# A hybrid encoder on one core: first activations on ScalarE's queue in two transfers, first weight pieces back to back on SyncE's, eight warm-up matmuls for eleven

## The chip, the core and the metric

The kernel runs on one NeuronCore of a Trainium2 chip. The core has five engines, each with its own instruction queue: TensorE (matmuls, with weight loads beside them), VectorE, ScalarE, GpSimd and SyncE, which here issues most of the DMAs. A DMA can be issued from the queue of SyncE, ScalarE or GpSimd; the issuing engine spends some time on it, and the transfer then runs on the core's DMA engines. The metric is the device time of one execution in microseconds.

## The reference

The input is 256 positions of width 2048, in float32. Two layers follow one another, each a token mixer and a gated MLP with residual adds, and a final RMS norm.

```python
h = x
for i in range(DEPTH):                        # DEPTH = 2
    hn = rms_norm(h, mix_norm[i])
    if i % 2 == 0: h = h + mixer_a(hn, ...)   # GQA, 16 query and 4 key heads, rotary
    else:          h = h + mixer_b(hn, ...)   # 3 groups of 8 heads, dilated windows
    h = h + conv_ffn(rms_norm(h, ffn_norm[i]), w_up, conv_w, conv_b, w_down)
return rms_norm(h, final_norm)
```

What matters here is the very first piece of this: the query, key and value projection of mixer A, `qkv = rms_norm(x) @ w_qkv` with a weight of 2048 x 3072. The kernel applies the norm's gain to x beforehand and its per-position factor after the projection, so the projection can begin as soon as some of x and some of the weight have been loaded.

## The kernel before

All matmuls of the projections compute a float32 product from parts: each operand is split into a high part, rounded to the matmul's input format, and a low part, the remainder. Three matmuls per tile are added up (high by high, high by low, low by high). The high part is a copy on ScalarE, the low part a subtraction on VectorE.

The activations come transposed from memory (`xT`, 128 partitions x 16 k-tiles x 256 positions). `load_xT(n)` loads four k-tiles, and `prep(j)` makes one k-tile's two parts: `split_scaled` on line 194 (ScalarE, the tile called xh in the profile) and line 197 (VectorE, the low part, under the same name). The weight comes in tiles of 512 x 512, that is 128 partitions x 2048 values or 1 MB. `feed` (line 121) loads one such tile (`raw`) and splits it in two halves, on line 146 (ScalarE, `wh`) and line 147 (VectorE, `wl`); lines 134 to 136 are its 24 matmuls, two blocks of 128 positions for each of four k-tiles, three matmuls each. Three `raw` buffers and three pairs of `wh` and `wl` go round.

`project2` computes the key block (n = 4) and the value block (n = 5) together, so that the first k-tiles of both can be used as they arrive. It passes a hook to `feed`. The first two tiles of each block are loaded in four pieces of 256 KB, the others in two of 512 KB, and the hook decides what is loaded beside them: for the first block, `load_xT(0)` to `load_xT(2)`, then parts of x and its sums of squares.

Within `feed` the splits of the weight are put into a high-priority block (`AHEAD`, 45 places), with which the framework's scheduler moves them ahead of work written earlier in the program. The order on each engine's queue is the one that results from that. For the first tile, the hook returns a function `mid`, which `feed` calls after each of its four pieces; `mid` issues the next activation piece and splits the present one.

Before all this, line 270 fills a tile with zeros and line 273 issues NWARM matmuls on it, whose result is not used. ScalarE's queue begins with the DMA of the gains (line 49) and a dummy activation (line 50, with the load of its function table ahead of it); GpSimd's has the DMA of an identity matrix (line 51).

Of the kernel before, what the change touches and what calls it, by code (L numbers as in the profile page):

```python
# [21 lines left out]
SCALE = 128.0 ** -0.5  # L22
NRAW, NHL = 3, 3
AHEAD = 45
NWARM = 11


@with_exitstack
def tile_encoder(ctx: ExitStack, tc: tile.TileContext, x, xT, w_a, w_ao, q_gain, k_gain, w_b, w_bo,
                 rel_bias, gains, w_up, conv, w_down, final_norm, rope, ident_c, onehot, out):  # L30
    nc = tc.nc
# [24 lines left out]
    def nm(s):  # L56
        uid[0] += 1
        return f"{s}_{uid[0]}"

    def ps_tile():  # L60
        return psp.tile([P, 512], F32, tag="ps", name=nm("ps"))
# [131 lines left out]
    def split_scaled(hi, lo, src, sc):  # L193
        nc.scalar.activation(hi, src, AF.Copy, scale=sc)
        if lo is None:
            return
        nc.vector.scalar_tensor_tensor(lo, src, sc, hi.bitcast(F32), ALU.mult, ALU.subtract)
# [15 lines left out]
    def new_hT(kt):  # L213
        t = hpool.tile([P, 2 * NT], F32R, tag=f"x{kt}", name=nm("xh"))
        return t[:, :NT], t[:, NT:], t
# [55 lines left out]
    wps = ps_tile()  # L271
    for _ in range(NWARM):
        nc.tensor.matmul(wps, warm[:, 0, :P], warm[:, 0, :], start=True, stop=True)
# [227 lines left out]
    def mixer_a():  # L501
        with tc.tile_pool(name="apool", bufs=1) as ap:
# [24 lines left out]
            def load_xT(n):  # L527
                xt = ap.tile([P, 4, NT], F32, tag=("qTh", "qTl", "vh", "vl")[n], name=nm("xt"))

                def load(j0, j1):  # L530
                    nc.sync.dma_start(xt[:, j0:j1, :], xT[:, 4 * n + j0:4 * n + j1, :])

                def prep(j):
                    kt = 4 * n + j
                    hT[kt] = new_hT(kt)
                    split_scaled(*hT[kt][:2], xt[:, j, :], gain[:, 0, kt:kt + 1])

                if n > 0:
                    load(0, 4)
                    for j in range(4):  # L540
                        prep(j)
                    return None
                load(0, 1)

                def mid(i):
                    if i < 3:
                        load(i + 1, i + 2)
                    prep(i)

                return mid  # L550

            def load_x(n):
                nc.sync.dma_start(h[:, :, n * 512:(n + 1) * 512],
# [3 lines left out]
            def hook(first_block, kg):  # L557
                if first_block and kg < 3:
                    return load_xT(kg)
                elif first_block:  # L560
                    load_x(2)
                    load_x(3)
                    rstd.append(finish_rstd(ss_in))
                elif kg == 0:
                    load_xT(3)
                elif kg == 1:
                    load_x(0)
                    tables()
                elif kg == 2:
                    load_x(1)  # L570
# [350 lines left out]
```

## Time and profile before

| | |
|---|---|
| median of 3 runs | 2316.41 us (2316.36 to 2316.6) |
| the profiled execution | 2316.06 us |
| its span, first to last instruction | 2313.9 us |
| TensorE busy (share of the span) | 2296.3 us (99%) |
| VectorE busy | 1603.5 us (69%) |
| ScalarE busy | 1199.2 us (52%) |
| bytes moved by DMA | 437.45 MB, mean 189 GB/s |

Times in the profile are microseconds from the start of the span. A row of the timeline has start, duration, engine, line, operation, what it writes and reads, how often; in brackets, how long the engine had been idle before and what ended that. "PE" is TensorE's matmul, "DVE" VectorE, "ACT" ScalarE, "POOL" GpSimd, "SPq" a DMA issue on SyncE's queue, "ACTq" one on ScalarE's. The chain of waits goes back from the last instruction, at each step to what released it. Matmuls overlap in the array: a row's 0.39 us is its whole way through, while the next one starts 0.23 us later. A row of a table of stretches has the stretch, its length, the busy time and number of instructions of TensorE, the weight load, VectorE, ScalarE and GpSimd, and then the granted clock, the share of time that the DMA engines were busy, and GB/s.

### The profile page before, as it was taken

Reading aid. Unit: us, or ns where it says so; the run is one execution under the profiler, and the core shown is the slowest. Engines: PE = TensorE matmul, PEld = TensorE weight load, DVE = VectorE, ACT = ScalarE, POOL = GpSimd, SP = SyncE. Lnnn points to the kernel's source line nnn. Section 1 sums busy time; section 2 is a strip of 40 time slices with the busy share of each in tenths; the row PEclk is TensorE's granted clock in tenths of the full one; section 3 lists DMA queues with packets and bytes.
Section 4 is the critical chain, followed back from the end, with each engine's and each line's share of the span. In section 5 each row is a group of like instructions: output and inputs, shape, how many; then the busy total and the mean of one; then the engine's idle time right before and its main releaser. Section 6 shows DMA issues by size and latency. Waiting matters only on the chain.

```text
span 2313.9 us, 30001 instructions
## 1 busy us (share of the span) xinstructions
PE 2296.3 (99%) x11641; PEld 1941.8 (84%) x11641; DVE 1603.5 (69%) x2197; ACT 1199.2 (52%) x1658; POOL 189.3 (8%) x143
## 2 busy tenths in 40 slices
PE   9999999999999999999999999999999999999997
PEld 7888788888888888888888888888888888888886
DVE  6877877775457776878866885677777744677754
ACT  6565465554345554545454554445555533555543
POOL 2330010100001010010000000001010100001010
PEclk9999999999999999999999999999999999999999
DMA  8434565765555555566555554556555555555553
GB/s 299 164 130 162 192 203 192 230 197 184 199 187 182 195 182 192 189 210 210 182 181 179 185 182 164 182 191 210 185 182 187 184 196 197 182 190 182 193 195 133
DMA packets 229023, 437.45 MB, mean 189 GB/s; under 512 B 10400, under 2 KB 193440, under 8 KB 201104
## 3 DMA queue, kind: packets, MB, share of 16 engines
q1 hardware_dynamic: 226976, 429.82, 55.1%
q0 software_dynamic: 1472, 5.15, 0.7%
q8 instruction: 91, 1.49, 0.3%
q10 hardware_dynamic: 432, 0.56, 0.1%
q14 instruction: 52, 0.43, 0.1%
HBM read 429.20 MB, written 6.29 MB: 188 GB/s over the span
## 4 chain that ended last, share of the span: by engine, by line
PE 92%; DVE 6%; issue 1%; ACT 1%; DMA 0%; SPq 0%; POOL 0%; POOLq 0%; DVEq 0%; ACTq 0%
PE acc L116 28%; PE acc L135 15%; PE acc L136 15%; PE acc L134 15%; PE acc L117 14%; DVE wl L147 2%; DVE tT L231 2%; PE ps L202 1%; PE ps L204 0%; PE ps L205 0%; PE ps L206 0%; PE ps L799 0%; DVE ro L583 0%; PE ps L653 0%; DVE ssq L591 0%
## 5 line engine op out<-in xcount | busy, mean ns | idle before, releaser
L116 PE MATMUL acc<-xh,wh 128*128 128x512 f32 x2816 | 994.2, 399 | 0.1
L117 PE MATMUL acc<-xh,wl 128*128 128x256 f32 x2816 | 789.3, 280 | 0.0
L147 DVE TENSOR_TENSOR wl<-raw,wh 128x1024 fp32r<-128x1024 f32 (+1 forms) x456 | 553.7, 1216 | 331.9 <-ACT wh L146 328.2
L146 ACT ACTIVATE wh<-raw 128x1024 fp32r<-128x1024 f32 (+1 forms) x456 | 475.6, 1045 | 551.8 <-PE acc L136 512.0
L116 PEld LDWEIGHTS acc<-xh,wh 128*128 128x128 f32 x2816 | 529.3, 188 | 130.6 <-DVE v L346 0.7
L111 DVE TENSOR_TENSOR wl<-raw,wh 128x1024 fp32r<-128x1024 f32 x352 | 431.1, 1225 | 207.1 <-ACT wh L110 202.9
L110 ACT ACTIVATE wh<-raw 128x1024 fp32r<-128x1024 f32 x352 | 372.5, 1059 | 327.0 <-PE acc L116 222.8
L117 PEld LDWEIGHTS acc<-xh,wl 128*128 128x128 f32 x2816 | 531.4, 189 | 1.0 <-issue 0.5
L135 PE MATMUL acc<-wl,ah 128*128 128x512 f32 x1024 | 399.6, 390 | 1.5 <-DVE wl L147 1.3
L134 PE MATMUL acc<-wh,ah 128*128 128x512 f32 x1024 | 399.3, 390 | 0.0
L136 PE MATMUL acc<-wh,al 128*128 128x512 f32 x1024 | 398.7, 389 | 0.0
L134 PE MATMUL acc<-wh,xh 128*128 128x512 f32 x768 | 303.1, 395 | 0.7 <-ACT wh L146 0.7
L135 PE MATMUL acc<-wl,xh 128*128 128x512 f32 x768 | 300.0, 391 | 0.2 <-DVE wl L147 0.2
L136 PE MATMUL acc<-wh,xh 128*128 128x512 f32 x768 | 299.3, 390 | 0.0
L135 PEld LDWEIGHTS acc<-wl,ah 128*128 128x128 f32 x1024 | 192.3, 188 | 43.7 <-DVE wl L147 4.6
L136 PEld LDWEIGHTS acc<-wh,al 128*128 128x128 f32 x1024 | 192.3, 188 | 39.7
L134 PEld LDWEIGHTS acc<-wh,ah 128*128 128x128 f32 x1024 | 192.3, 188 | 39.5
L365 POOL TENSOR_TENSOR cv<-cg,cv 128x512 f32<-128x512 f32 x44 | 98.8, 2245 | 1166.5 <-ACT wh L110 907.4
L136 PEld LDWEIGHTS acc<-wh,xh 128*128 128x128 f32 x768 | 144.2, 188 | 30.1
L135 PEld LDWEIGHTS acc<-wl,xh 128*128 128x128 f32 x768 | 144.4, 188 | 28.8 <-DVE wl L147 1.7
L134 PEld LDWEIGHTS acc<-wh,xh 128*128 128x128 f32 x768 | 144.5, 188 | 28.5 <-ACT wh L146 1.1
L190 ACT ACTIVATE ah<-cv 128x256 fp32r<-128x256 f32 x88 | 32.0, 410 | 108.8 <-POOL cv L365 108.8
(151 smaller groups left out, 1375.0 us busy)
## 6 DMA issues: line engine op xcount, KB each, us to landing
raw<-in_w_up_dram SPq DMA_DIRECT2D x352, 512.0 KB
raw<-in_w_down_dram SPq DMA_DIRECT2D x88, 1024.0 KB
raw<-in_w_b_dram SPq DMA_DIRECT2D x72, 1024.0 KB
raw<-in_w_bo_dram SPq DMA_DIRECT2D x24, 1024.0 KB
raw<-in_w_a_dram SPq DMA_DIRECT2D x16, 1024.0 KB
raw<-in_w_ao_dram SPq DMA_DIRECT2D x16, 1024.0 KB
raw<-in_w_a_dram SPq DMA_DIRECT2D x16, 256.0 KB
raw<-in_w_a_dram SPq DMA_DIRECT2D x8, 512.0 KB
```

Source lines behind the costliest of these rows:

```text
L110: nc.scalar.activation(wh, rk, AF.Copy)
L111: nc.vector.tensor_tensor(wl, rk, wh.bitcast(F32), ALU.subtract)
L116: nc.tensor.matmul(acc[j], wh[:, kt, c], x, start=first and i == 0 and kt == 0, stop=False)
L117: nc.tensor.matmul(acc[j][:, :NT], wl[:, kt, c], x[:, :NT], start=False, stop=last and i == len(kgs) - 1 and kt == 3)
L134: nc.tensor.matmul(accs[m], xh[:, c], wh[:, j, :], start=st, stop=False)
L135: nc.tensor.matmul(accs[m], xh[:, c], wl[:, j, :], start=False, stop=False)
L136: nc.tensor.matmul(accs[m], xl[:, c], wh[:, j, :], start=False, stop=sp)
L146: nc.scalar.activation(wh[:, c], r[:, c], AF.Copy)
L147: nc.vector.tensor_tensor(wl[:, c], r[:, c], wh[:, c].bitcast(F32), ALU.subtract)
L190: nc.scalar.activation(hi, src, AF.Copy)
L231: nc.vector.transpose(o[cols].rearrange("p a (m t) -> p a m t", m=2)[:, :, :, rows], s[rows].rearrange("p m (a c) -> p a m c", c=P)[:, :, ...
L365: nc.gpsimd.tensor_tensor(cv, cg, cv, ALU.mult)
```

## The change

`load_xT(0)` no longer loads its four k-tiles one by one, each between two weight pieces, on SyncE's queue. It issues them all at once from ScalarE's queue: the first k-tile (128 KB), then the other three in one transfer (384 KB). The function that `feed` calls after each weight piece is now `prep` alone, so the four weight pieces stand one behind the other on SyncE's queue. The calls of `prep` come in the same places as before; where the splits end up on ScalarE and VectorE is left to the scheduler. The warm-up has eight matmuls instead of eleven. The later tiles' loads keep their queue.

```diff
-NWARM = 11
+NWARM = 8
...
-                def load(j0, j1):
-                    nc.sync.dma_start(xt[:, j0:j1, :], xT[:, 4 * n + j0:4 * n + j1, :])
+                def load(j0, j1, q=nc.sync):
+                    q.dma_start(xt[:, j0:j1, :], xT[:, 4 * n + j0:4 * n + j1, :])
...
-                load(0, 1)
-
-                def mid(i):
-                    if i < 3:
-                        load(i + 1, i + 2)
-                    prep(i)
-
-                return mid
+                load(0, 1, nc.scalar)
+                load(1, 4, nc.scalar)
+                return prep
```

## The prediction

> **What bounds the kernel now.** I read the page first (busy shares and the chain that ended last), then the chain of waits over the first 50 us, then the timeline of the first 12 us.
>
> ```profile
> PE 2296.3 (99%) x11641; PEld 1941.8 (84%) x11641; DVE 1603.5 (69%) x2197; ACT 1199.2 (52%) x1658; POOL 189.3 (8%) x143
> ...
> PE 92%; DVE 6%; issue 1%; ACT 1%; DMA 0%; SPq 0%; POOL 0%; POOLq 0%; DVEq 0%; ACTq 0%
> ```
>
> TensorE is busy 99% of the span and 92% of the chain. Whatever delays its unbroken stream of matmuls at the start is paid once, in full, at the end, unless a later pause of TensorE takes it up. The edit touches only the start, so the question is when that stream begins.
>
> ```profile
> 1.66 0.42 SPq L531
> ...
> 2.12 5.11 DMA raw<-in_w_a_dram
> ...
> 7.26 0.64 ACT wh L146
> ...
> 7.92 0.70 DVE wl L147
> ...
> 8.67 0.50 PE acc L135
> 9.17 0.23 PE acc L136
> ...
> 45.59 0.24 PE acc L136
> ```
>
> This is the chain by time. The second weight piece, issued by SyncE at 2.12 us behind two activation pieces, lands at 7.23; its high part (ScalarE) and low part (VectorE) follow, and from 8.67 on the chain is one matmul after another, 0.23 us apart, up to 45.8 us. The timeline shows what came before that.
>
> ```profile
> 0.74 0.41 ACTq L49 DMA_DIRECT2D gain<-in_gains_dram  x1
> ...
> 1.46 4.28 PE L273 MATMUL ps<-warm 128*128 128x512 f32 x11 [1.46 <-DVE warm L270]
> ...
> 2.47 0.21 ACT L50 ACTIVATE act<-nhalf 128x8 f32<-128x8 f32 x1
> ...
> 3.28 0.51 ACT L194 ACTIVATE xh<-xt,gain 128x256 fp32r<-128x256 f32 x1 [0.60 <-DMA gain<-in_gains_dram]
> ...
> 3.82 0.48 DVE L197 SCALAR_TENSOR_TENSOR xh<-xt,gain,xh 128x256 fp32r<-128x256 f32 x1 [2.42 <-ACT xh L194]
> ...
> 4.42 0.63 ACT L146 ACTIVATE wh<-raw 128x512 fp32r<-128x512 f32 x1 [0.63 <-DMA raw<-in_w_a_dram]
> ...
> 5.08 0.69 DVE L147 TENSOR_TENSOR wl<-raw,wh 128x512 fp32r<-128x512 f32 x1 [0.78 <-ACT wh L146]
> ...
> 5.57 0.40 PE L134 MATMUL acc<-wh,xh 128*128 128x512 f32 x1
> ...
> 7.94 0.50 PE L134 MATMUL acc<-wh,xh 128*128 128x512 f32 x1 [0.69 <-ACT wh L146]
> ...
> 10.59 0.91 ACT L194 ACTIVATE xh<-xt,gain 128x256 fp32r<-128x256 f32 x2 [0.65 <-DMA xt<-in_xT_dram]
> ```
>
> Six real matmuls run from 5.57, a seventh at 7.94, then the stream from 8.67. So the stream stands as if it had begun at 8.67 - 7 x 0.23 = 7.06 us. That is the figure to beat.
>
> **The change part by part.** (1) Order of the work. In the changed program's instruction order ScalarE no longer alternates xh (activation) and wh (weight): after the dummy activation come two DMA issues, then all four wh pieces of the first weight tile, and only then the four xh. VectorE likewise has all four wl ahead of the first low part. TensorE's order is the same but for three warm-ups. The first matmul needs the first xh, so it now waits, through ScalarE's order, for the fourth weight piece; before, it waited for one activation piece and one weight piece. What is queued behind the waiting instruction is all of ScalarE, with VectorE's low parts and TensorE behind that.
>
> (2) When that piece lands.
>
> ```profile
> raw<-in_w_a_dram SPq DMA_DIRECT2D x10, 256.0 KB
> xt<-in_xT_dram SPq DMA_DIRECT2D x3, 512.0 KB
> ...
> xt<-in_xT_dram SPq DMA_DIRECT2D x4, 128.0 KB
> ident<-in_ident_dram POOLq DMA_DIRECT2D x1, 64.0 KB, 4.3
> ...
> 3.00:5.50 2.50, 2.50 (x9) 1.97 (x8) 0.90 (x2) 1.14 (x2) 0.00 (x0) 1.00 0.78 202
> 7.50:10.50 3.00, 2.33 (x9) 1.71 (x10) 2.69 (x6) 2.44 (x5) 0.00 (x0) 1.00 1.04 385
> ```
>
> (The last two rows are stretches of the span; their last column is GB/s.) The fourth transfer, 128 + 256 + 128 + 256 = 768 KB into SyncE's queue, lands at 7.23; the ninth, 2048 KB in, lands at 10.59, where xh of the second tile stops waiting. That is 1280 KB in 3.36 us, 381 KB per us, in agreement with the 385 GB/s row. The first 1536 KB, the same four activation and four weight pieces that the changed kernel loads first, are in at 7.23 + 768/381 = 9.25 us. The changed kernel has the weights alone on SyncE's queue from 0.74 us; the activations (128 and 384 KB) start after the dummy activation, at 2.68, two issues of 0.41 us. I take it that they share the transfer time with the weights about equally, so that weight piece four is near the end of the 1536 KB: 9.25. The two ends: 9.6, if the activations go first throughout, and 6.1, if the slow 202 GB/s up to 5.5 us was the fault of the interleaved small pieces: the first weight piece landed at 4.42 with 384 KB in, and 640 KB more at 381 KB per us make 6.1. I keep near the upper end, because the slow stretch is a time of low rate for every transfer in it, and the transfer of ident on GpSimd's queue, which takes 4.3 us to land and lies in it, stays.
>
> (3) From the landing to the matmul: wh 0.63, xh 0.51 and some 0.05 of hand-over: 9.25 + 1.19 = 10.44 us. The other three wh and wl lie under the wait. Against 7.06 the stream is 3.38 us late. The low part of xh (0.48, after the last wl of 0.69) is ready at about 11.1; the third matmul wants it at 10.9 at full clock, 11.3 at the slow one below, so it costs 0.2 or nothing.
>
> (4) The warm-ups and the clock.
>
> ```profile
> 2.05 3.69 PE L273 MATMUL ps<-warm 128*128 128x512 f32 x10
> ...
> 4.61 1.13 PE L273 MATMUL ps<-warm 128*128 128x512 f32 x4
> ...
> 5.11 0.62 PE L273 MATMUL ps<-warm 128*128 128x512 f32 x2
> ...
> 2301.70 0.39 PE L136 MATMUL acc<-wh,al 128*128 128x512 f32 x1
> 2304.00:2305.00 1.00, 0.00 (x0) 0.00 (x0) 0.83 (x5) 0.00 (x0) 0.66 (x1) 1.00 0.00 0
> 2305.00:2306.00 1.00, 0.00 (x0) 0.00 (x0) 0.66 (x1) 0.66 (x2) 0.30 (x1) 0.63 0.00 0
> ```
>
> From 2.05 to 4.61 six warm-ups start, 0.427 us each; from 5.11 to the first real matmul at 5.57 two, 0.23 each. TensorE thus runs at about half rate until some 3.3 us after its first matmul at 1.46. At the end of the kernel the last matmul ends at 2302.1, the granted clock (third column from the right) is still 1.00 in the second to 2305 and 0.63 in the next, so it fell to half at 2305.26, 3.2 us after. The three warm-ups removed are the last ones, at full clock: 0.69 us of TensorE that nobody waited for, since the second weight piece is late; removing them saves nothing. Eight warm-ups end at 4.9; then TensorE idles until 10.44, 5.5 us, more than the 3.2 after which the clock fell at the end. So the stream starts at half rate. I take the 3.3 us of the first start: 3.3 x (1 - 0.23/0.427) = 1.52 us lost. Bounds: nothing, if the clock holds or returns at once, and 6.6 us of slow running, 3.0 us lost.
>
> (5) SyncE's queue loses four issues of about 0.42; the next tile's activations go out right behind the four weight pieces, and the following pieces earlier. Nothing waits for them: TensorE needs the second tile 24 matmuls, 5.5 us, after its start. Cost and gain nothing, and if that cover were gone it would be the 0.65 us wait at 10.59.
>
> (6) Later, ScalarE has one wh before the two evacuations of the k projection (it stood between them), and the last step of the k transposes one place earlier.
>
> ```profile
> 45.92 0.69 ACT L468 ACTIVATE stg<-acc,rstd 128x512 f32<-128x512 f32 x1 [1.72 <-PE acc L136]
> ...
> 46.51 1.05 ACT L146 ACTIVATE wh<-raw 128x1024 fp32r<-128x1024 f32 x1
> ...
> 67.62 1.06 ACT L146 ACTIVATE wh<-raw 128x1024 fp32r<-128x1024 f32 x1 [1.66 <-PE acc L136]
> ...
> 72.21 2.08 ACT L146 ACTIVATE wh<-raw 128x1024 fp32r<-128x1024 f32 x2
> ...
> 74.19 1.25 ACT L468 ACTIVATE stg<-acc,rstd 128x512 f32<-128x512 f32 x2
> ...
> 74.94 5.59 POOL L588 TENSOR_TENSOR t<-stg,st_q 128x256 f32<-128x256 f32 x4 [19.07 <-ACT stg L468]
> ...
> 81.85 1.09 PE L485 MATMUL ps<-ident,ro 128*128 128x128 f32 x8 [0.55 <-DVE ro L594]
> ```
>
> VectorE's work there moves up by about 0.6 us (46.51 to 45.92). But the only pause of TensorE that follows, 0.55 at 81.85, hangs on GpSimd's 5.59 us, which start with the evacuation at 74.19; ahead of it stands a wh that waits for TensorE's own pace (24 x 0.23 = 5.5 us after the one released at 67.62, so 73.1, and it ran from 73.25). At most 0.2 us can be won; taken as nothing. The pause is tied to TensorE's progress, so it takes up none of the delay.
>
> Sum: 3.38 + 1.52 = 4.9 us. The profiled execution took 2316.06 (span 2313.9 and 2.2 around it), so it would take 2320.96; the median of the runs is 2316.41, 0.35 above it, and the forecast is 2321.3, slower by 0.21%.
>
> **The rivals.** *The clock counts in fixed stretches.* Both delays seen, 3.15 to 3.4 us up and 3.2 down, fit a gate that judges stretches of some 3.3 us that begin where they will. A start amid a stretch would then be slow for the rest of it and the whole next one, 5.0 us in the mean: 2.3 lost, +5.7, 2322.1. Against it: one start and one end are all the trace has. The Trainium skill ("TensorE: Matmul & The Clock Gate", Part 1: The HAM clock gate) states this: the clock opens after one busy window and closes after one idle window, each about 3.4 us, and the window runs free of the kernel. The trace agrees in both delays; by that page the loss would be 1.6 to 3.1 and the sum 5.0 to 6.5.
>
> *The clock does not fall, or returns at once:* 3.38 + 0.2 = +3.6, 2320.0. For it: the early rows say 1.00 even while the warm-ups run at 0.427, so the row is no proof of the state there. Against it: the end of the kernel.
>
> *The two queues do not share.* If weights pass first, 1024 KB are in at 7.23 + 256/381 = 7.9, the stream begins at 9.1, +2.0 and 1.5 for the clock: +3.5, 2319.9. For it: nothing but their head start of 2 us. The Trainium skill ("DMA: Bandwidth & Descriptors", Issuing engines are not separate DMA queues) says that transfers from all issuing engines run on the same 16 engines and interleave, which speaks for the 9.25; no run here shows it yet.
>
> *Not slower.* If the 202 GB/s stretch goes with the small pieces, weight four lands at 6.1, the first matmul starts at 7.3 with its third waiting some 0.2 for the low part, and TensorE has idled only 2.4 us, so the clock holds: +0.4, 2316.8. It decides from a landing below about 5.7 on; even 0.6 us sooner gains only 0.2. For it: the engines were busy only 0.78 in that stretch. Against it: ident and the gains lie there as before.
>
> **How the numbers follow.** Forecast case 0.50 (its own range 2320.3 to 2322.2), fixed stretches 0.15, clock holds 0.08, no sharing 0.14, not slower 0.11, anything in the later order 0.02. About 0.2% (4.6 us, to 2321.04) is what a measurement of this kernel can tell from no change. Above it lie some 0.31 of the forecast case, 0.14 of the fixed stretches and 0.02 of the rest: slower 0.47. Faster by that much needs a gain that no step has: 0.03. The rest, 0.50, is within. The range leaves out most of the not-slower case and the top of the fixed stretches: 2317.6 to 2322.9.
>
> **What would show it.** Step 1: the first xh directly behind four wh, VectorE's first low part behind four wl. Step 2: the fourth wh starts at 9.25 (8.5 to 9.6 is right; below 7.5 the forecast falls). Step 3: the first real matmul at about 10.4. Step 4: eight warm-ups to 4.9, first real ones 0.43 apart, 0.23 apart some 3 to 5 us later, and a clock below 1.00 in rows between 8 and 14 us. Step 6: the pause near 87 us still about 0.55. It would be wrong if the weights land early, or if a wait that the trace of before does not have takes the place of these.

## The result, and the profile after

| | before | after |
|---|---|---|
| median of 12 runs each | 2315.41 us (2309.56 to 2317.89) | 2320.5 us (2319.57 to 2322.76) |
| the profiled execution | 2316.06 us | 2319.8 us |
| its span | 2313.9 us | 2318.0 us |

The changed kernel is slower: the ratio is 1.0025, 95% interval 1.0017 to 1.0033. TensorE is still busy 99% of the span, as the busy shares and the shares of the chain that ended last on the changed kernel's page show, so a microsecond lost at the start is again a microsecond of the time.

```profile
PE 2295.9 (99%) x11638; PEld 1941.5 (84%) x11638; DVE 1604.1 (69%) x2197; ACT 1198.7 (52%) x1658; POOL 190.6 (8%) x143
...
PE 93%; DVE 5%; issue 1%; ACT 1%; DMA 0%; SPq 0%; POOL 0%; POOLq 0%; DVEq 0%; ACTq 0%
```

The chain of the changed kernel's first 20 us (start, length, what) has one long link in it, the fourth weight piece, issued at 2.12 and landing 6.62 us later, at 8.74.

```profile
2.12 6.62 DMA raw<-in_w_a_dram
```

Before, the link at this place was the second piece, landing at 7.23. The timeline of the changed kernel says how the engines stood meanwhile.

```profile
0.74 1.81 SPq L125 DMA_DIRECT2D raw<-in_w_a_dram  x4
...
1.18 1.28 ACT L50 ACT_TABLE_LOAD   x1 [1.18 <-PEq L905]
1.24 0.88 ACTq L531 DMA_DIRECT2D xt<-in_xT_dram  x2
...
1.46 3.61 PE L273 MATMUL ps<-warm 128*128 128x512 f32 x8 [1.46 <-DVE warm L270]
...
8.10 1.29 ACT L146 ACTIVATE wh<-raw 128x512 fp32r<-128x512 f32 x2 [2.37 <-DMA raw<-in_w_a_dram]
...
9.30 1.69 ACT L194 ACTIVATE xh<-xt,gain 128x256 fp32r<-128x256 f32 x4
9.85 0.80 PE L134 MATMUL acc<-wh,xh 128*128 128x512 f32 x1 [4.79 <-ACT xh L194]
...
15.07 0.40 PE L134 MATMUL acc<-wh,xh 128*128 128x512 f32 x1
```

ScalarE makes all four `wh` and only then the first `xh`, on which the first matmul waits 4.79 us. The thirteenth matmul stands at 15.07, so the first twelve took 5.22 us. At the full pace of 0.23 they would have taken 2.76. The table of stretches of the changed kernel (the stretch, its length, busy time of TensorE, weight load, VectorE, ScalarE and GpSimd; granted clock, DMA share, GB/s) shows why. The stretches are 3.41 us long, and cut so that the changes of the granted clock (4.74, 8.15 and 14.98) fall on their edges. Ahead of the first change in a profile the clock's column reads 1.00 whatever the pace is; there the spacing of the matmuls tells the clock, 0.43 us at half and 0.23 at full.

```profile
1.33:4.74 3.41, 3.28 (x8) 2.48 (x8) 0.07 (x1) 1.92 (x3) 0.72 (x1) 1.00 0.75 212
4.74:8.15 3.41, 0.32 (x2) 0.00 (x0) 1.39 (x2) 0.73 (x3) 0.00 (x0) 1.00 0.98 351
8.15:11.57 3.42, 1.72 (x4) 1.40 (x5) 2.81 (x6) 3.39 (x8) 0.00 (x0) 0.50 1.05 400
11.57:14.98 3.41, 3.41 (x9) 2.64 (x9) 2.52 (x6) 1.66 (x4) 0.00 (x0) 0.50 1.03 389
```

The clock opened at 4.74, while the last of the eight warm-ups was running (they end at 5.07). The next stretch is almost idle (0.32 of 3.41), and at 8.15 the clock falls to half. In the stretch from 8.15 TensorE begins to work in its middle and the clock stays at half for one more, fully busy stretch. It is full again only at 14.98: two stretches, 6.83 us.

There is a second loss, much later. Here is the changed kernel's timeline around 76 us, and the rows of the kernel before that answer to it.

```profile
75.88 1.06 ACT L190 ACTIVATE kTh<-tT 128x1024 fp32r<-128x1024 f32 x1 [5.13 <-DVE tT L231]
76.85 2.94 ACT L146 ACTIVATE wh<-raw 128x1024 fp32r<-128x1024 f32 x3
...
76.98 1.22 DVE L191 TENSOR_TENSOR kTl<-tT,kTh 128x1024 fp32r<-128x1024 f32 x1 [1.13 <-ACT kTh L190]
78.12 3.49 DVE L147 TENSOR_TENSOR wl<-raw,wh 128x1024 fp32r<-128x1024 f32 x3
...
79.39 0.50 PE L135 MATMUL acc<-wl,xh 128*128 128x512 f32 x1 [0.94 <-DVE wl L147]
...
87.58 1.09 PE L485 MATMUL ps<-ident,ro 128*128 128x128 f32 x8
```

```profile
71.25 1.06 ACT L190 ACTIVATE kTh<-tT 128x1024 fp32r<-128x1024 f32 x1 [2.57 <-DVE tT L231]
...
71.25 1.23 DVE L147 TENSOR_TENSOR wl<-raw,wh 128x1024 fp32r<-128x1024 f32 x1
72.39 1.22 DVE L191 TENSOR_TENSOR kTl<-tT,kTh 128x1024 fp32r<-128x1024 f32 x1
```

Before, one weight split more stood ahead of the k transposes' copy: VectorE did that `wl` at 71.25 and `kTl` after it, and two `wh` were queued behind `kTh`. Now three are, and the first of their `wl` comes after `kTl`, at 78.12, just too late for TensorE, which waits 0.94 us at 79.39. In return the pause of 0.55 at the eight transposes of line 485 is gone. These stood at 81.85 before and stand at 87.58 now: the stream is 5.73 us behind. I use this row as the mark for every kernel below, because it lies behind both losses: from here to 440 us the changed kernel stays between 5.7 and 5.9 us behind. What comes later, down to the 4.1 us by which the spans differ, happens in one stage whose pace the edit does not decide (last section).

### The profile page after: what moved, and what is told of

Same layout as the page of the kernel before. It is cut to its first block, busy times and chain, and to the rows that moved or that the text cites. A ratio compares the mean times of both kernels' runs of the same rounds, so it can differ in the third digit from the quotient of the medians.

```text
span 2318.0 us, 29988 instructions
## 1 busy us (share of the span) xinstructions
PE 2295.9 (99%) x11638; PEld 1941.5 (84%) x11638; DVE 1604.1 (69%) x2197; ACT 1198.7 (52%) x1658; POOL 190.6 (8%) x143
## 4 chain that ended last, share of the span: by engine, by line
PE 93%; DVE 5%; issue 1%; ACT 1%; DMA 0%; SPq 0%; POOL 0%; POOLq 0%; DVEq 0%; ACTq 0%
PE acc L116 28%; PE acc L135 16%; PE acc L136 16%; PE acc L134 16%; PE acc L117 14%; DVE wl L147 2%; DVE tT L231 2%; PE ps L202 1%; PE ps L204 0%; PE ps L205 0%; PE ps L206 0%; PE ps L794 0%; DMA raw<-in_w_a_dram 0%; PE ps L648 0%; DVE h L285 0%
```

## The experiments

The first four runs were timed beside 33 runs of the kernel before, median 2313.35 us; the last four, on another chip, beside 15, median 2315.89. The rows come from one profiled execution each.

**Warm-ups alone.** The kernel before with eight warm-ups.

```diff
-NWARM = 11
+NWARM = 8
```

> The kernel before, with eight warm-up matmuls instead of eleven and nothing else. Theory (removed warm-ups cost nothing, since the second weight piece at 7.2 us is what TensorE waits for): first real matmul at 5.1 instead of 5.57, the stream of matmuls still from 8.67, the clock stays up, the transposes after the q projection at 81.9, time as before within 0.1%. Rival (a gate that judges fixed stretches of 3.4 us): the stretch from 4.7 to 8.1 us is now only half busy; if that is too little, the clock falls at 8.1 and the next 3.4 us run at 0.43 a matmul: 1.6 us later from there on, +0.07%.

Measured: 2313.15 us, ratio 1.0002 (0.9992 to 1.0012). The timeline, then two stretches of this run:

```profile
5.49 0.79 PE L134 MATMUL acc<-wh,xh 128*128 128x512 f32 x1 [0.25 <-ACT wh L146]
...
10.60 0.39 PE L136 MATMUL acc<-wh,xh 128*128 128x512 f32 x1
...
82.75 1.09 PE L485 MATMUL ps<-ident,ro 128*128 128x128 f32 x8 [0.56 <-DVE ro L594]
```

```profile
3.70:7.12 3.42, 3.17 (x7) 1.75 (x6) 1.64 (x3) 1.69 (x4) 0.00 (x0) 1.00 0.88 264
7.12:10.53 3.41, 3.41 (x9) 2.64 (x9) 2.20 (x5) 2.22 (x5) 0.00 (x0) 1.00 1.00 333
```

The first matmul starts at 5.49, as early as before (5.57), but the clock does not open until 10.53: eleven matmuls, most of them 0.43 apart, fill the 5.11 us to 10.60. The stream is 0.90 us behind at the mark. The 3.41 us up to 7.12, which hold the gap from the last warm-up to the first matmul and its slow start, did not open the clock. So without the three warm-ups the clock may be left at half for a stretch more. The 0.90 is no fixed price: the kernel before itself varies by 0.72 at the mark (below), and in the time of the whole kernel it can't be seen.

**Many warm-ups.** The changed kernel with 29.

```diff
-NWARM = 8
+NWARM = 29
```

> The changed kernel, with 29 warm-up matmuls, so that TensorE has work from 1.5 until the first real matmul at 9.85. Theory (the cold start costs 2.5 us of the change): real matmuls 0.23 us apart from the first on, the clock rows 1.00 from 4.7 us on, the thirteenth real matmul at 12.6 instead of 15.07, everything after it 2.4 us sooner than in the changed kernel; time some 0.1% below it, still above the kernel before. Rival (the slow matmuls cost nothing, since something else sets the pace of the first 15 us): the sixteenth and later matmuls wait for wh, wl or xh, and at 20 us nothing is gained.

Measured: 2318.37 us, ratio 1.0015 (1.0006 to 1.0024).

```profile
1.46 8.44 PE L273 MATMUL ps<-warm 128*128 128x512 f32 x29 [1.46 <-DVE warm L270]
10.88 0.50 PE L134 MATMUL acc<-wh,xh 128*128 128x512 f32 x1 [0.98 <-ACT xh L194]
...
86.47 1.09 PE L485 MATMUL ps<-ident,ro 128*128 128x128 f32 x8
```

The clock holds and the matmuls come 0.23 apart from the fourth on. The weight landed late in this run, so that the first matmul is 1.03 us behind that of the changed kernel (9.85), and yet the mark is 1.11 ahead of it (87.58). The clock's part is thus about 2.1 us, where I had expected 2.4. The rest, 86.47 - 81.85 = 4.62, is landing and late order.

**Order at the start.** The changed kernel with the splits of the first activations moved ahead, between the weight splits.

```diff
-                    split_scaled(*hT[kt][:2], xt[:, j, :], gain[:, 0, kt:kt + 1])
+                    if n > 0:
+                        split_scaled(*hT[kt][:2], xt[:, j, :], gain[:, 0, kt:kt + 1])
+                        return
+                    with tc.high_priority(offset=2 * AHEAD):
+                        split_scaled(*hT[kt][:2], xt[:, j, :], gain[:, 0, kt:kt + 1])
```

> The changed kernel with the transfers as they are, but the first tile's activation splits given a higher priority than its weight splits: ScalarE then does wh, wh, xh, wh, xh, xh, xh, wh. Theory (ScalarE's order, not the transfers, delays the first matmul): the first activations landed by about 5.4, so the first matmul starts at about 6.3, the stream from 9.2 with six matmuls done, 0.8 us behind the kernel before, clock up throughout; 4.3 us sooner than the changed kernel at 20 us. Rival (the transfers are late): the first matmul is hardly earlier than 9.

Measured: 2314.13 us, ratio 1.0001 (0.9992 to 1.0011).

```profile
6.27 0.80 PE L134 MATMUL acc<-wh,xh 128*128 128x512 f32 x1 [1.03 <-ACT xh L194]
...
10.01 0.80 PE L134 MATMUL acc<-wh,xh 128*128 128x512 f32 x1 [0.82 <-ACT xh L194]
...
77.59 0.51 PE L135 MATMUL acc<-wl,xh 128*128 128x512 f32 x1 [0.93 <-DVE wl L147]
...
85.78 1.09 PE L485 MATMUL ps<-ident,ro 128*128 128x128 f32 x8
```

The first matmul no longer hangs on the fourth piece: it starts 3.58 us sooner than in the changed kernel. Only 1.80 of that is left at the mark. Six matmuls are possible, then the second k-tile's `xh` stands behind the third `wh`, whose weight piece lands at 8.9, so TensorE stops again until 10.01, and the clock stays at half until 13.87. The late wait is the same as the changed kernel's (0.93). So my expectation held for the first matmul, but not for the stream, which I saw 0.8 behind the kernel before with the clock up throughout: at the mark it is 3.93 behind. In the median it can't be told from the kernel before. The two readings do not agree, and the last section says what spoils the median.

**Late order.** The changed kernel with 44 places for the high-priority block. This leaves the first 20 us as they are and puts the instructions from 46 to 76 us back into the order of the kernel before.

```diff
-AHEAD = 45
+AHEAD = 44
```

> The changed kernel with AHEAD 44 instead of 45. On all five queues this puts the work from 46 to 76 us back into the order that it has in the kernel before (the first copy of the k evacuation ahead of one weight split, the last copy of the k transposes behind one), and leaves the start as changed. Theory (the later order costs 0.7 us: a new wait of 0.94 at 79.4 us against a pause of 0.55 that goes): no wait at 79.4, the pause ahead of the transposes is back at about 0.55, and what follows is 0.7 us sooner than in the changed kernel. Rival (that wait comes from the late start and not from the order): it stays.

Measured: 2316.92 us, ratio 1.0014 (1.0005 to 1.0023).

```profile
10.67 0.80 PE L134 MATMUL acc<-wh,xh 128*128 128x512 f32 x1 [5.43 <-ACT xh L194]
...
87.31 1.09 PE L485 MATMUL ps<-ident,ro 128*128 128x128 f32 x8 [0.54 <-DVE ro L589]
```

There is no wait near 79 us, and the pause of 0.54 at the transposes is back. The landing is late in this run too: the first matmul is 0.82 behind the changed kernel's, and the mark 0.27 ahead. To take the start out, I count from one matmul behind it, the 55th of the projection, in the kernel before, the changed kernel and this run:

```profile
19.82 0.39 PE L134 MATMUL acc<-wh,xh 128*128 128x512 f32 x1
```

```profile
24.61 0.39 PE L134 MATMUL acc<-wh,xh 128*128 128x512 f32 x1
```

```profile
25.28 0.39 PE L134 MATMUL acc<-wh,xh 128*128 128x512 f32 x1
```

The changed kernel is 4.79 us behind there and this run 5.46. From there to the mark the changed kernel loses 0.94 more (5.73), this one nothing (5.46). So the late order costs 0.94 us net, where I had expected 0.7: the wait of 0.94 and shorter stops about it, less the pause of 0.55.

**The same programs again.** Both kernels, unchanged.

> The kernel before, unchanged, profiled once more. If the clock is judged in stretches whose phase is the run's own, its clock opens at some other point than 4.69 us, anywhere from about 3.5 to 8 us, and the first matmuls are 0.23 or 0.43 us apart accordingly; if the start alone decides, it opens at 4.69 again. If the two paces of the 512-column and 256-column matmuls are a property of the run and not of the edit, the stretch from 441 to 534 us or from 1594 to 1829 us may come out about 2 or 4 us shorter than in the first profile of the same program; if they belong to the program, both come out as before, to 0.2 us.

> The changed kernel, unchanged, profiled once more. By the landing theory the first matmul follows the fourth weight piece by about 1.1 us whatever the landing is, and the landing differs by up to 1 us from 8.74 (first matmul between 9.3 and 10.9). By the theory of fixed stretches the clock is open by 5.2 at the latest or stays shut, closes before the first matmul or shortly after it, and the slow matmuls last until 13 to 17.5 us. The wait of about 0.9 us near 79 us is there again, as it is a matter of order. The rival, that the end of the slow matmuls is tied to the first matmul, has it 5.1 us behind the first matmul again.

Measured, in one run each: before 2315.81 us, after 2319.87 us. First the timeline of the kernel before, second time, then that of the changed kernel with the stretch that opened its clock.

```profile
6.31 0.39 PE L134 MATMUL acc<-wh,xh 128*128 128x512 f32 x1
...
82.57 1.09 PE L485 MATMUL ps<-ident,ro 128*128 128x128 f32 x8 [0.55 <-DVE ro L594]
```

```profile
10.34 0.80 PE L134 MATMUL acc<-wh,xh 128*128 128x512 f32 x1 [5.45 <-ACT xh L194]
...
79.48 0.50 PE L135 MATMUL acc<-wl,xh 128*128 128x512 f32 x1 [0.92 <-DVE wl L147]
...
87.67 1.09 PE L485 MATMUL ps<-ident,ro 128*128 128x128 f32 x8
```

```profile
0.95:4.36 3.41, 2.90 (x7) 2.32 (x8) 0.45 (x1) 1.59 (x3) 0.76 (x2) 1.00 0.71 184
```

The kernel before opened its clock at 4.69 in the first profile and at 6.28 in this one, where all eleven warm-ups ran slowly and the first matmul stood behind them until 6.31: 0.72 behind at the mark, by chance alone. The changed kernel opened at 4.36, fell to half at 7.77 and was full again at 14.60; it landed half a microsecond later and still has the mark within 0.1 of the first time, since its clock came back 0.38 sooner. The end of the slow matmuls is therefore not tied to the first matmul, as the rival had it: it comes 14.60 - 10.34 = 4.26 us behind it, against 14.98 - 9.85 = 5.13 in the first profile. The wait at 79 us is there again (0.92). The first matmul is 10.34 - 8.60 = 1.74 us behind the start of the third `wh` (8.60 in this run), and 9.85 - 8.10 = 1.75 in the first profile: what varies is the landing.

**The queue.** The changed kernel, with its two activation transfers on SyncE's queue, ahead of the weights.

```diff
-                load(0, 1, nc.scalar)
-                load(1, 4, nc.scalar)
+                load(0, 1)
+                load(1, 4)
```

> The changed kernel with its two activation transfers issued by SyncE, ahead of the four weight pieces; eight warm-ups. It tells whether ScalarE's queue matters for the landing. If all queues share one rate (381 KB per us and the slow first 5 us), the fourth weight piece lands as in the changed kernel, 8.7 give or take 0.5, since the same 1536 KB are asked for, though SyncE issues them 0.9 us later. If a second queue brings a rate of its own, it lands 1 us later or more, at 9.8 or above. As the splits of the activations stand ahead of the first weight split here, the first matmul no longer hangs on the fourth piece but on the first, which lands behind 512 KB of activations: I expect the first matmul at 6.3 to 7.0 us, and the stream, counted from the first matmul that nothing delays any more, some 2 us sooner than the changed kernel's.

Measured: 2318.56 us in one run.

```profile
6.88 0.50 PE L134 MATMUL acc<-wh,xh 128*128 128x512 f32 x1 [1.64 <-ACT wh L146]
...
7.13 2.00 ACT L146 ACTIVATE wh<-raw 128x512 fp32r<-128x512 f32 x3
...
83.42 1.09 PE L485 MATMUL ps<-ident,ro 128*128 128x128 f32 x8 [0.55 <-DVE ro L589]
```

```profile
5.42:8.83 3.41, 1.73 (x6) 1.22 (x7) 2.86 (x6) 3.29 (x7) 0.00 (x0) 1.00 1.04 376
8.83:12.24 3.41, 3.41 (x9) 2.64 (x9) 1.90 (x4) 1.74 (x5) 0.00 (x0) 0.50 0.96 354
```

Three `wh` follow one another from 7.13 without a wait, so the fourth piece was in by 7.13 + 2 x 0.67 = 8.46, no later than with ScalarE's queue (8.74). In this profile a second queue brought no rate. That is what the Trainium skill says ("DMA: Bandwidth & Descriptors", Issuing engines are not separate DMA queues): transfers of all issuing engines run on the same DMA engines. What the queue did change is the scheduler's order: here three of the four `xh` stay ahead of the first `wh`, the late order is the old one, and the mark is 4.16 us sooner than the changed kernel's (87.58 - 83.42). I had expected some 2. The clock's loss remains: a stretch busy for 1.73 of 3.41 us sent it to half for the next.

**A start meant to beat both.** SyncE issues the first k-tile and then the four weight pieces; ScalarE the second k-tile, and then the other two in one transfer; the order of the splits is close to the old one, and twelve warm-ups.

```diff
-NWARM = 8
+NWARM = 12
...
-                load(0, 1, nc.scalar)
-                load(1, 4, nc.scalar)
+                load(0, 1)
+                with tc.high_priority(offset=5):
+                    load(1, 2, nc.scalar)
+                    load(2, 4, nc.scalar)
...
-                    split_scaled(*hT[kt][:2], xt[:, j, :], gain[:, 0, kt:kt + 1])
+                    if n > 0:
+                        split_scaled(*hT[kt][:2], xt[:, j, :], gain[:, 0, kt:kt + 1])
+                        return
+                    with tc.high_priority(offset=AHEAD):
+                        split_scaled(*hT[kt][:2], xt[:, j, :], gain[:, 0, kt:kt + 1])
```

> Meant as a version that beats both: SyncE issues the first activation k-tile and then the four weight pieces back to back; ScalarE issues the second k-tile and then the third and fourth in one transfer; the splits of the first tile's activations keep their place between the weight splits, as in the kernel before; twelve warm-ups, so that TensorE is busy without a gap until the first split is there. If the landing and the order of the splits are all there is to the start, the fourth weight piece lands at 8.5 to 9 against 10.2 before, the first matmul starts at 5.5 to 6.7, and the stream stands as if begun at 6.0 to 7.0, so 0 to 1 us ahead of the kernel before at 20 to 400 us. The pause at 82 us stays (0.55) and no wait comes at 79, as the later order is that of the kernel before. In the medians of the runs that is too little to tell: ratio 0.9992 to 1.0003. If activation pieces that share the transfers with the weights delay the first weight piece, as they do in the kernel before, the stream begins no sooner: 0 to 0.5 us behind.

Measured: 2315.77 us, ratio 1.0000 (0.9991 to 1.0009).

```profile
8.75 0.50 PE L134 MATMUL acc<-wh,xh 128*128 128x512 f32 x1 [0.89 <-ACT xh L194]
...
11.66 0.50 PE L134 MATMUL acc<-wh,xh 128*128 128x512 f32 x1 [0.99 <-ACT xh L194]
...
83.43 1.09 PE L485 MATMUL ps<-ident,ro 128*128 128x128 f32 x8 [0.55 <-DVE ro L595]
```

My expectation was wrong. The clock holds, but TensorE stops twice: until 8.75 for an `xh` that stands behind the second weight piece, which landed only at 7.67, and until 11.66 for the last two activation k-tiles, which landed at 11.1. ScalarE had issued them only at 3.73, behind the first `xh`. At the mark it is 1.58 behind the first profile of the kernel before and 0.86 behind the second. No version tried here beats the kernel before.

## Why the prediction was right, and where it was not

The forecast was 2321.3 us, within 2317.6 to 2322.9; measured were 2320.5. The direction and most of the size came from the right places, but two terms were off in opposite directions and one step was wrong. That the forecast comes within 1 us of the median is partly luck: the stream was 5.73 us late at the mark and not 4.9, and the whole time also depends on a pace that the prediction knew nothing of (last section). Up to the mark, from the rows above:

| | predicted | in the changed kernel's profile |
|---|---|---|
| first matmul, against 7.06 | +3.38 | 9.85 - 7.06 = +2.79 |
| slow matmuls | +1.52 | 5.22 - 2.76 = +2.46 |
| late order | 0 | +0.94 (late-order run) |
| at the mark, 81.85 before | +4.9 | +5.73 |

The three measured terms make 6.19. The rest, -0.46, lies ahead of the matmul at 19.82 (2.79 + 2.46 = 5.25, but +4.79 there): small stops of the kernel before, ahead of 20 us, that the delay takes up.

1. *Order on ScalarE.* Right: the first matmul waited, through four `wh`, for the last weight pieces. With the splits moved ahead it came at 6.27.
2. *Landing at 9.25.* Right in kind, and 0.5 too late for this profile (8.74). That is within what varies by itself: with the same start the third `wh` began at 8.10 here, at 8.60 the second time, at 8.95 in the late-order run and at 9.15 with 29 warm-ups, and the first matmul came between 9.85 and 10.88, on both sides of the 10.44 predicted. One reading was wrong: I let the issue of the activations wait for the dummy activation at 2.68, and the row shows it at 1.24, beside the load of the function table. What that did to the landing is not shown. The rate in the early stretch rose:

```profile
3.00:5.50 2.50, 2.06 (x6) 1.23 (x4) 0.67 (x1) 1.02 (x2) 0.00 (x0) 1.00 0.92 288
```

That is 288 GB/s against 202 before (second profiles: 267 and 222), part of what the "not slower" rival supposed, but far from its landing at 6.1. Transfers shared the rate, as step 2 took it; the no-sharing rival is gone with the queue experiment.

3. *From landing to matmul.* 9.85 - 8.74 = 1.11, predicted 1.19.
4. *The clock.* It fell, as said, but the size was wrong by 0.9: I took the 3.3 us of a first start, and the clock was at half for 6.83, two whole stretches, of which 5.1 us fell on matmuls. The rival of fixed stretches, to which I gave 0.15, is what the runs show: changes came at multiples of 3.41 us from one another in every profile (4.74, 8.15 and 14.98; 4.36, 7.77 and 14.60; in the queue run 5.42, 8.83 and 12.24), and at another phase in each. The Trainium skill ("TensorE: Matmul & The Clock Gate", Part 1: The HAM clock gate) states a free-running window of 3413 ns, and the runs agree. That removing the three warm-ups "saves nothing" was right. That nobody needed them is doubtful: without them, in the one profile of the warm-ups-alone run, the clock was at half until 10.53, whereas with them it opened at 4.69 and 6.28.
5. *SyncE's shorter queue.* Nothing gained or lost in any row.
6. *The later order.* Wrong. I saw that one `wh` and one transpose had changed places, asked only what could be gained, and expected the pause at the transposes to stay. It went, and a wait of 0.94 us came 8 us ahead of it. The step had said that the last step of the k transposes (`kTh` and `kTl`) comes one place earlier, and not asked how much later the `wh` and `wl` that now stand behind it would be.

The whole time differs by 5.1 us in the medians and 3.7 in the profiled executions, 5.73 at the mark. The difference between mark and end is explained below.

## What to carry to other kernels

When a load moves to another engine's queue, look first at what the scheduler makes of the order on that engine: here the last weight piece landed no later from SyncE's queue alone than from two queues (8.46 against 8.74 us, in one profile each), but the order that came with it put the mark 4.2 us sooner (the queue run). A gap of TensorE that closes the clock must be priced in whole clock stretches (3.41 us each, phase unknown), and warm-ups are worth having up to the moment at which the first real matmul is sure to follow (29 of them instead of eight gave 2.1 us here). When instructions change places far from the edit, work out the lateness of each, not only what may be gained.

## What the runs showed that I had not expected

*Two paces of the same matmuls.* In the second half of the up-projection (441 to 534 us) and in one later stage (1594 to 1829 us), the same pairs of a 512-column and a 256-column matmul (lines 116 and 117) run at one of two paces, TensorE being busy all the time at full clock. The tables of stretches count them. First the kernel before, then the kernel before a second time, then the late-order run:

```profile
450.00:530.00 80.00, 80.00 (x454) 69.39 (x454) 58.36 (x80) 44.44 (x61) 9.08 (x4) 1.00 0.57 186
```

```profile
450.00:530.00 80.00, 80.00 (x463) 70.57 (x462) 59.06 (x81) 45.85 (x62) 8.89 (x4) 1.00 0.58 188
1600.00:1800.00 200.00, 200.00 (x1134) 173.33 (x1133) 145.39 (x197) 112.61 (x151) 20.30 (x9) 1.00 0.57 188
```

```profile
1600.00:1800.00 200.00, 200.00 (x1156) 174.83 (x1155) 147.63 (x201) 113.69 (x153) 21.97 (x10) 1.00 0.58 191
```

454 against 463 matmuls in the same 80 us, 1134 against 1156 in 200: 2% each, or some 1.8 us over the first stage and 4.5 over the second. The same program had either pace in the first stage, so the edit does not decide it. In the second stage three of the four experiments on the first chip were fast, and all four profiles on the second were slow. This is what lies between mark and end: the changed kernel's profile had the fast pace in the first stage where that of before had the slow one, and wins back 1.8 of its 5.7 us there. Matched matmul by matmul, the changed kernel is 5.86 us behind just ahead of that stage (445.93 against 440.07), 3.90 just behind it (545.05 against 541.15) and 3.93 at the last matmul (2305.63 against 2301.70). Together the two stages would account for some 6 of the 8 us over which the runs of the kernel before spread. They blur the medians of the experiments by more than the marks differ, so I go by the marks. What chooses the pace was not found. Nor was what cost the queue run about 1 us more between 415 and 441 us.

*What the clock gate counts as busy.* By busy time, stretches with 2.90 to 3.41 us opened the clock. One with 3.17 did not (warm-ups alone, 3.70 to 7.12). One with 1.73 closed it (the queue experiment), while stretches of 2.52 and 2.43 in the last experiment, with its two stops, left it open. So a half-busy stretch counts as idle, and the profile's busy time does not decide near the border; I leave open what does.
